# A convolution mixer taken by two halves of the tokens, with one of six convolution tiles moved off TensorE and half of its second product in whole fp32

## The chip, the core and the metric

The kernel runs on one core of one Trainium2 chip. The metric is the device time of one execution in microseconds; the median of several runs counts. Everything is in fp32, with fp32r (one pass through TensorE instead of several) for the large products.

## The reference, cut to what matters

The reference is a trunk of four layers on 256 tokens of 1024 channels. Each layer adds a token mixer and then a squared-ReLU feed-forward network (FFN) of 4096. Only the mixer of layer 1, a Conformer convolution module, is changed:

```
h = xn @ pw1_w + pw1_b
a, gate = split(h, 2);  h = a * sigmoid(gate)
h = causal depthwise convolution of width 31 (h, dw_w) + dw_b
h = layer_norm(h, ln_w, ln_b)          # over the 1024 channels of a token
h = silu(h)
x = x + h @ pw2_w + pw2_b
x = x + squared_relu_mlp(rms_norm(x))  # the FFN of layer 1 follows
```

## The kernel before

Activations lie channels on partitions: eight tiles of 128 channels by 256 tokens. Weights come from memory in chunks of 1 MB, two units of 128 x 1024 to a chunk, through three buffers (`raw`). `unit` splits a unit into a high fp32r part (a copy on ScalarE, line 350) and the rest (a subtraction on VectorE, line 351). A product is then three fp32r matmuls for each pair of a weight block and an activation tile (lines 470 to 472 in `mm_b`): high by high, high by low, low by high. Activations are split in the same way (`split`, lines 362 and 363).

The mixer is `conv`. After the first product and the gate, the eight gated tiles (`hc`) stand in SBUF with 31 columns of zeros ahead. Their depthwise convolution is done in two ways:

- Tile 0 on VectorE, one fused multiply-add for each of 31 taps (line 982); tile 1 on ScalarE (a scaled copy for each tap, line 989) with GpSimd adding (line 991). Both are over before TensorE begins its own tiles.
- Tiles 2 to 7 on TensorE (`taps_pe`, line 995). `spread` writes two tiles at a time to a scratch in device memory (`hd`, line 912) and reads them back so that 32 channels by 4 shifts lie on the 128 partitions (line 915, into a `raw` buffer). Thirty-two matmuls in fp32, each of 32 columns of weights by 256 tokens, then make a tile; four of them stand side by side in the array's columns.

For the layer norm, each finished tile gets a common shift taken off (line 1045) and is squared on ScalarE (line 1004). `stats` sums tiles 0 to 5 by channels with 32-column matmuls (line 1009); `cols` then turns the sums and tiles 6 and 7 into a column for each token (line 387). Mean and scale are worked out in small VectorE steps, and `bcast` (line 394) spreads them over the partitions again. `warm` puts idle bf16 matmuls on TensorE meanwhile (line 291). `swish` normalizes on VectorE (lines 1100 and 1101) and applies SiLU on ScalarE (line 1103). The second product is `out_proj`, and its results are added to `x` (line 868), from which `norm_pair` makes the FFN's inputs `z` (line 418).

Order: within this stage PE, DVE, ACT and POOL keep the order in which the code is written (`manual_schedule`); elsewhere a scheduler decides. All DMAs are issued from SP's queue, in order. The release of `raw` buffers sets when weights load: all three hold `spread` tiles during the taps.

Of the kernel before, what the change touches and what calls it, by code (L numbers as in the profile page):

```python
# [39 lines left out]
PET = (2, 3, 4, 5, 6, 7)  # L40
DVT = (0, 1)
# [200 lines left out]
class Trunk:  # L242
# [81 lines left out]

    def unit(self, key, after=None):
# [19 lines left out]
        with ExitStack() as stack:  # L345
            for i in after or ():
                stack.enter_context(self.tc.issue_after(i.ins))
            for i in range(0, 1024, n):
                s = slice(i, i + n)
                nc.scalar.copy(hi[:, s], src[:, s])  # L350
                nc.vector.tensor_sub(lo[:, s], src[:, s], hi[:, s])  # L351
        self.un += 1
        return hi, lo

# [4 lines left out]
    def split(self, src, eng="act"):  # L359
        nc = self.nc  # L360
        o = self.bigt(F32R)
        (nc.scalar.copy if eng == "act" else nc.vector.tensor_copy)(o[:, :S], src)  # L362
        self.last_lo = nc.vector.tensor_sub(o[:, S:], src, o[:, :S])
        return o
# [177 lines left out]
    def res_pairs(self, name, l, acts, nkb, group, evac, before=None, after=None):  # L542
        for g in range(4 // group):
            ps = [self.acc() for _ in range(group)]
            for kb in range(nkb):
                if before is not None:
                    before(kb)
                for p in range(group):
                    w = self.unit((name, l, "b", kb, (g * group + p) * 256), after and after.pop(0))
# [305 lines left out]
    def out_proj(self, name, l, y, nkb, group, nxt, bias=None, before=None, after=None):  # L855
        nc = self.nc

        acts = lambda k: y[k]
# [15 lines left out]
        self.res_pairs(name, l, acts, nkb, group, evac, before, after)  # L874
# [16 lines left out]
    def conv(self, j, nxt):  # L891
# [17 lines left out]
        def spread(d):  # L909
            rows = self.dram.tile([2, 4, 32, HL], F32, name=self.nm("hd"), tag="hd")  # L910
            for i in range(2):
                nc.sync.dma_start(rows[i].rearrange("j c u -> (j c) u"), hc[d + i][:, :HL])
            t = self.raw.tile([P, RAWW], F32, name=self.nm("raw"), tag="raw")
            for s in range(4):
                nc.sync.dma_start(
                    v3(t[32 * s : 32 * s + 32], 8, HW),
                    rows.rearrange("i j c u -> c (i j) u")[:, :, NG * s : NG * s + HW],
                )
            for i in range(2):
# [40 lines left out]
        spread(6)  # L960
        self.table("silu_and_others")
        tap = lambda t, w: hc[t][:, w + 1 : w + 1 + S]
# [4 lines left out]
        halves = lambda t: (t()[:, :S], t()[:, :S])  # L967
        r0, r1 = halves(self.mis), halves(self.bigt)
        pb, pbs = {}, [self.acc() for _ in range(3)]
        for i, d in enumerate(PET):  # L970
            pb[d] = pbs[i % 3][:, (i // 3) * S : (i // 3 + 1) * S]


        def tap_dve(t, w, a, first=False, bias=False):
            if bias:
                nc.vector.tensor_scalar(
                    out=a, in0=tap(t, w), scalar1=wc(t, w), scalar2=db(t), op0=ALU.mult, op1=ALU.add
                )
            elif first:
                nc.vector.tensor_scalar(out=a, in0=tap(t, w), scalar1=wc(t, w), scalar2=None, op0=ALU.mult)  # L980
            else:
                nc.vector.scalar_tensor_tensor(out=a, in0=tap(t, w), scalar=wc(t, w), in1=a, op0=ALU.mult, op1=ALU.add)

        def tap_pool(t, w, a, first=False, bias=False):
            pr = a if first else self.prp.tile([P, S], F32, name=self.nm("pr"), tag="pr")
            if bias:
                nc.scalar.activation(out=pr, in_=tap(t, w), func=AF.Identity, scale=wc(t, w), bias=db(t))
            else:
                nc.scalar.activation(out=pr, in_=tap(t, w), func=AF.Copy, scale=wc(t, w))
# [13 lines left out]
        def square(d):  # L1003
            L["sq", d] = nc.scalar.activation(out=cc[d][:, S:], in_=cc[d][:, :S], func=AF.Square)

        def stats(*ds):
            for d in ds:
                o = 32 * (d % 4)
                nc.tensor.matmul(L["st"][o : o + 32], self.c("o32", 32), cc[d], start=d < 4, stop=d in (2, 3, 4, 5), **kw)


        def cols(src, sc, es=(0, 1), first=False, last=False):
            for e in es:
                for t in range(2):
                    i = t * 2 + e
                    self.colsum(
                        L["sc"][:, i : i + 1], src[:, e * S + t * P : e * S + (t + 1) * P], self.sc(sc),
                        first and i == 0, last,
                    )
# [10 lines left out]
        def shift_b():  # L1030
            s0 = self.col(2, "lns")
            nc.vector.tensor_copy(s0, L["ps"][:, :2])
            L["s"] = self.bcast(s0, "Gb")
            L["st"] = self.mis()
# [9 lines left out]
        def fin_pe(d):  # L1044
            L["fin", d] = nc.vector.scalar_tensor_tensor(
                out=cc[d][:, :S], in0=pb[d], scalar=db(d), in1=L["s"], op0=ALU.add, op1=ALU.subtract
            )
            square(d)

        with self.tc.manual_schedule(engines=MANUAL):  # L1050
# [4 lines left out]
            taps_pe(2)  # L1055
            shift_a()
            taps_pe(3)
            shift_b()
            shift_c()
            square(1)  # L1060
            fin(0, *r0)
            square(0)
            fin_pe(2)
            fin_pe(3)
            taps_pe(4)
            fin_pe(4)
            taps_pe(5)
            fin_pe(5)
            stats(0, 1, 2, 3)
            taps_pe(6)  # L1070
            fin_pe(6)
            stats(4, 5)
            sm, L["sc"] = self.tmp(), self.mis()
            nc.scalar.copy(sm, L["st"])
            taps_pe(7)
            fin_pe(7)
            cols(sm, 128, first=True)
            cols(cc[6], 1024)
            cols(cc[7], 1024, (0,))
            cols(cc[7], 1024, (1,), last=True)  # L1080

            mean, msq = v3(L["sc"][:, :4], 2, 2)[:, :, 0], v3(L["sc"][:, :4], 2, 2)[:, :, 1]
            mc, m2, m = self.col(2, "lnc"), self.col(2, "lnm2"), self.col(2, "lnm")
            nc.vector.tensor_copy(mc, mean)
            self.warm(2)
            mb = self.bcast(mc, "lnb", 1)
            self.warm(2)
            nc.vector.tensor_mul(m2, mc, mc)
            nc.vector.scalar_tensor_tensor(out=m, in0=msq, scalar=EPS, in1=m2, op0=ALU.add, op1=ALU.subtract)
            rs = self.rsqrt(m, 2, "v")  # L1090
            rsb = self.bcast(rs, "lnr", 1)
            self.warm(9)
            y, yp = [], {}

            def swish(d):
                c = cc[d][:, :S]
                if d % 4 == 0:
                    for e in range(d, d + 4):
# [219 lines left out]
```

## Time and profile before

| | us |
|---|---|
| median of 3 runs | 1375.63 (1375.15 to 1376.71) |
| the profiled execution | 1373.77 |
| its span, first to last instruction | 1372.0 |
| TensorE busy in the span | 1357.4 (99%) |
| VectorE busy | 978.4 (71%) |
| ScalarE busy | 770.9 (56%) |
| GpSimd busy | 136.0 (10%) |

An fp32 matmul stands in the profile as two records, so that a tile of 32 tap matmuls shows as x64. TensorE's records overlap: from start to start of two neighbours is what one costs, and it is shorter than a record's own duration. "PEclk" is the granted TensorE clock as a share of 2.4 GHz. The convolution's part that is changed lies between 438 and 512 us of the span.

### The profile page before, as it was taken

To read this page: it belongs to the slowest core of one execution; us is meant where nothing else is said; L and a number is where in the kernel's file an instruction comes from. 1 tells how busy PE (TensorE), PEld (TensorE's weight loads), DVE (VectorE), ACT (ScalarE), POOL (GpSimd) and SP (SyncE) were. 2 spreads that over 40 slices of the span, in tenths; PEclk is the share of its full clock that TensorE was granted. 3 is DMA by queue.
4 is the path that set the end of the run, shared out by engine and by line. 5 is a ranking of instruction groups with operands and counts; after the bars stand their busy time and mean duration, and the time that the engine had idled before them with its cause. 6 is when DMAs were issued, how large, how long until landed. Compare 5 with 4: busy or idle time off the path is not lost.

```text
span 1372.0 us, 22537 instructions
## 1 busy us (share of the span) xinstructions
PE 1357.4 (99%) x9057; PEld 1224.0 (89%) x9058; DVE 978.4 (71%) x1653; ACT 770.9 (56%) x1155; POOL 136.0 (10%) x125
## 2 busy tenths in 40 slices
PE   9999999999999989999999999999999999999998
PEld 7889998888999678888988898888988999988888
DVE  6967778775678588765588587756597687888543
ACT  7545556664456366654568666644565554655442
POOL 2201002000227010000000010000120010100011
PEclk9999999999999999999999999999999999999999
DMA  8543445555455555555543345555554444455550
GB/s 304 210 166 141 152 163 202 184 190 195 170 183 121 160 191 192 196 185 184 184 156 142 133 159 184 197 196 185 182 179 165 150 158 171 168 193 188 191 187 37
DMA packets 38649, 239.93 MB, mean 175 GB/s; under 512 B 4240, under 2 KB 8720, under 8 KB 10896
## 3 DMA queue, kind: packets, MB, share of 16 engines
q1 hardware_dynamic: 38256, 237.97, 49.8%
q8 instruction: 71, 1.16, 0.3%
q10 hardware_dynamic: 288, 0.52, 0.1%
q14 instruction: 34, 0.28, 0.1%
HBM read 236.54 MB, written 1.93 MB: 174 GB/s over the span
## 4 chain that ended last, share of the span: by engine, by line
PE 96%; DVE 2%; DMA 1%; ACT 1%; issue 0%; SPq 0%; POOL 0%; ACTq 0%; DVEq 0%; POOLq 0%
PE acc L497 32%; PE acc L498 16%; PE acc L472 9%; PE acc L470 9%; PE acc L471 9%; PE acc L887 4%; PE acc L886 4%; PE acc L888 4%; PE acc L995 2%; PE mis L387 1%; DMA raw<-in_w 1%; PE mis L394 1%; DVE wl L351 1%; PE acc L486 1%; PE acc L484 1%; PE acc L485 1%
## 5 line engine op out<-in xcount | busy, mean ns | idle before, releaser
L351 DVE TENSOR_TENSOR wl<-raw,wh 128x1024 fp32r<-128x1024 f32 (+1 forms) x444 | 552.1, 1247 | 283.2 <-ACT wh L350 278.1
L350 ACT CAST wh<-raw 128x1024 fp32r<-128x1024 f32 (+1 forms) x444 | 460.6, 1041 | 428.1 <-PE acc L497 207.4
L497 PE MATMUL acc<-z,wh 128*128 128x512 f32 x1120 | 391.8, 395 | 4.1 <-DVE z L418 4.1
L498 PE MATMUL acc<-z,wl 128*128 128x256 f32 x1120 | 312.6, 281 | 0.0
L497 PE MATMUL acc<-big,wh 128*128 128x512 f32 x768 | 267.7, 393 | 0.0
L497 PEld LDWEIGHTS acc<-z,wh 128*128 128x128 f32 x1120 | 209.2, 187 | 52.3 <-DVE z L418 5.2
L498 PE MATMUL acc<-big,wl 128*128 128x256 f32 x768 | 215.2, 280 | 0.0
L498 PEld LDWEIGHTS acc<-z,wl 128*128 128x128 f32 x1120 | 211.6, 189 | 1.0
L497 PEld LDWEIGHTS acc<-big,wh 128*128 128x128 f32 x768 | 143.8, 187 | 32.7
L472 PE MATMUL acc<-big,wl 128*128 128x256 f32 x576 | 162.1, 283 | 0.6 <-DVE wl L351 0.6
L471 PE MATMUL acc<-big,wh 128*128 128x256 f32 x576 | 161.6, 283 | 0.0
L470 PE MATMUL acc<-big,wh 128*128 128x256 f32 x576 | 160.5, 284 | 0.0
L472 PE MATMUL acc<-z,wl 128*128 128x256 f32 x512 | 145.2, 284 | 0.5 <-DVE wl L351 0.5
L470 PE MATMUL acc<-z,wh 128*128 128x256 f32 x512 | 145.4, 284 | 0.0
L498 PEld LDWEIGHTS acc<-big,wl 128*128 128x128 f32 x768 | 145.2, 189 | 0.0
L471 PE MATMUL acc<-z,wh 128*128 128x256 f32 x512 | 144.9, 283 | 0.0
L433 POOL TENSOR_TENSOR t<-t,t 128x512 f32<-128x512 f32 x25 | 38.3, 1532 | 763.5 <-DVE z L418 459.8
L472 PEld LDWEIGHTS acc<-big,wl 128*128 128x128 f32 x576 | 110.3, 192 | 0.8 <-DVE wl L351 0.8
L471 PEld LDWEIGHTS acc<-big,wh 128*128 128x128 f32 x576 | 110.3, 192 | 0.0
L470 PEld LDWEIGHTS acc<-big,wh 128*128 128x128 f32 x576 | 109.1, 192 | 0.9 <-DVE big L362 0.4
L472 PEld LDWEIGHTS acc<-z,wl 128*128 128x128 f32 x512 | 98.1, 192 | 0.8 <-DVE wl L351 0.8
L471 PEld LDWEIGHTS acc<-z,wh 128*128 128x128 f32 x512 | 98.1, 192 | 0.0
(243 smaller groups left out, 1821.1 us busy)
## 6 DMA issues: line engine op xcount, KB each, us to landing
raw<-in_w SPq DMA_DIRECT2D x216, 1024.0 KB, 4.8
raw<-in_w SPq DMA_DIRECT2D x8, 512.0 KB, 8.6
raw<-hd SPq DMA_DIRECT2D x12, 263.0 KB, 4.7
x<-in_x SPq DMA_DIRECT2D x4, 256.0 KB, 6.3
hd<-big SPq DMA_DIRECT2D x6, 143.5 KB, 2.2
cst<-in_cst SPq DMA_DIRECT2D x4, 192.0 KB, 5.0
cst<-in_cst SPq DMA_DIRECT2D x1, 548.0 KB, 9.7
out<-t SPq DMA_DIRECT2D x2, 256.0 KB, 2.7
```

What stands on the lines that cost most here:

```text
L350: nc.scalar.copy(hi[:, s], src[:, s])
L351: nc.vector.tensor_sub(lo[:, s], src[:, s], hi[:, s])
L433: (nc.vector if p == 3 and self.quick else nc.gpsimd).tensor_add(a, self.sq, q)
L470: nc.tensor.matmul(o, wh[:, kk, cs], ah, start=st, stop=False, **kw)
L471: nc.tensor.matmul(o, wh[:, kk, cs], al, start=False, stop=False, **kw)
L472: nc.tensor.matmul(o, wl[:, kk, cs], ah, start=False, stop=en, **kw)
L497: nc.tensor.matmul(ps[m], wh[:, kk, cs], a, start=first and kk == 0, stop=False, **kw)
L498: nc.tensor.matmul(ps[m][:, :S], wl[:, kk, cs], a[:, :S], start=False, stop=last and kk == 3, **kw)
L886: nc.tensor.matmul(ps[t], zh[:, s], wh[:, kk], start=k == 0, stop=False, skip_group_check=True)
L887: nc.tensor.matmul(ps[t], zh[:, s], wl[:, kk], start=False, stop=False, skip_group_check=True)
L888: nc.tensor.matmul(ps[t], zl[:, s], wh[:, kk], start=False, stop=k == 7, skip_group_check=True)
L995: nc.tensor.matmul(pb[d][32 * j : 32 * j + 32], strip[d][g // 4][:, ((g % 4) * 4 + j) * 32 : ((g % 4) * 4 + j + 1) * 32], h4[d][:, j * HW ...
```

## The change

All tokens are taken as two halves of 128. Tile 7 leaves TensorE: VectorE computes its first half (`taps_7a`), ScalarE and GpSimd its second (`taps_7b`). The five tiles left on TensorE are computed by halves, all of the first half ahead of most of the second. The layer norm is done for each half by itself, so that the first half's statistics, broadcasts and SiLU are written between the second half's taps, and the second half's between matmuls of the second product. That product's first four k-tiles (the first half of its contraction) are no longer split in fp32r parts: their four weight units come straight from memory into eight 128 x 512 tiles (`unit_raw`), and 64 plain fp32 matmuls of 128 x 128 by 128 tokens (`mm_h`) take the place of 96 fp32r matmuls by 256 tokens. The last four k-tiles stay as they were. The idle matmuls of `warm` in this stage go.

```diff
-PET = (2, 3, 4, 5, 6, 7)
-DVT = (0, 1)
+PET = (2, 3, 4, 5, 6)
+DVT = (0, 1, 7)
...
+    def unit_raw(self, key, tiles):
+        assert PLAN[self.un] == key, (PLAN[self.un], key)
+        o = self.un % UPC * 1024
+        for t in tiles:
+            self.nc.sync.dma_start(t, self.w_d[self.un // UPC][:, o : o + 512])
+            o += 512
+        self.un += 1
+        return tiles
...
+    def bcast_1(self, c, tag):
+        nc = self.nc
+        ps = self.mis()
+        nc.tensor.matmul(ps[:, :P], c.to_broadcast([P, P]), self.id, start=True, stop=True)
+        b = self.bc.tile([P, P], F32, name=self.nm(tag), tag=tag, bufs=1)
+        nc.scalar.copy(b, ps[:, :P])
+        return b
...
-        spread(6)
+        spread(6, 1)
...
-        def taps_pe(d):
-            for g, j in ((g, j) for g in range(NG) for j in range(4)):
+        def taps_pe(d, h, gs=range(NG)):
+            for g, j in ((g, j) for g in gs for j in range(4)):
                 nc.tensor.matmul(
-                    pb[d][32 * j : 32 * j + 32], strip[d][g // 4][:, ((g % 4) * 4 + j) * 32 : ((g % 4) * 4 + j + 1) * 32],
-                    h4[d][:, j * HW + g : j * HW + g + S], start=g == 0, stop=g == NG - 1, **kw,
-                )
+                    pb[d][32 * j : 32 * j + 32, hs(h)],
+                    strip[d][g // 4][:, ((g % 4) * 4 + j) * 32 : ((g % 4) * 4 + j + 1) * 32],
+                    h4[d][:, hs(h, j * HW + g)], start=g == 0, stop=g == NG - 1, **kw,
+                )
...
+        def mm_h(p, kks, h):
+            for kk in kks:
+                w = v3(W[p][kk // 2], 2, 256)
+                for m in range(2):
+                    nc.tensor.matmul(
+                        ps[p][:, m * S : (m + 1) * S][:, hs(h)], w[:, kk % 2, m * P : (m + 1) * P], cc[kk][:, hs(h)],
+                        start=kk == m == h == 0, stop=False, **kw,
+                    )
...
-            taps_pe(2)
+            W = [self.unit_raw(key(0, p), [(self.tmp if p < 2 else self.bigt)() for _ in range(2)]) for p in range(4)]
+            taps_pe(2, 0)
             shift_a()
-            taps_pe(3)
+            taps_7a(range(4))
             shift_b()
...
+            taps_pe(3, 0)
+            shift_bb()
+            taps_7a(range(4, 11))
+            taps_pe(4, 0)
...
+            taps_pe(5, 0)
+            fin_pe(0, 5)
...
+            taps_pe(2, 1)
+            stats(0, 0, 1, 2, 3)
...
+            taps_pe(3, 1)
+            fin_pe(1, 3)
+            taps_7b(range(21, 23))
+            taps_pe(6, 0)
+            fin_pe(0, 6)
+            taps_pe(4, 1, range(4))
+            stats(0, 4, 5, 6, 7)
+            stats_out(0)
+            taps_7b(range(23, CW))
+            taps_pe(4, 1, range(4, NG))
+            cols_st(0, True)
+            mean_in(0)
+            taps_pe(5, 1, range(4))
+            mean_out(0)
+            scale_in(0)
+            swish_mean(0, 0, 1, 2, 3)
+            fin_7(1)
+            taps_pe(5, 1, range(4, NG))
+            stats(1, 0, 1, 2, 3)
+            scale_out(0)
+            fin_pe(1, 4, 5)
+            taps_pe(6, 1, range(4))
+            swish(0, 0, 1, 2, 3)
+            square(7, 1)
+            stats(1, 4, 5, 7)
+            stats_out(1)
+            taps_pe(6, 1, range(4, NG))
+            swish_mean(0, 4, 5, 6, 7)
+            fin_pe(1, 6)
+            swish(0, 4, 5)
+            ps = [self.acc() for _ in range(4)]
+            mm_h(0, range(2), 0)
+            cols_st(1, False)
+            mm_h(0, range(2, 3), 0)
+            cols_tile(1, 6, True)
+            mean_in(1)
+            mm_h(0, range(3, 4), 0)
+            mm_h(1, range(2), 0)
+            mean_out(1)
+            scale_in(1)
+            W1 = [self.unit(key(1, 0))]
+            swish_mean(1, 0, 1, 2, 3)
+            swish(0, 6, 7)
+            mm_h(1, range(2, 4), 0)
+            mm_h(2, range(3), 0)
+            scale_out(1)
+            mm_h(2, range(3, 4), 0)
+            mm_h(3, range(4), 0)
+            swish(1, 0, 1, 2, 3)
+            W1.append(self.unit(key(1, 1)))
+            for p in range(4):
+                mm_h(p, range(4), 1)
+            swish_mean(1, 4, 5, 6, 7)
+            swish(1, 4, 5, 6, 7)
+        evac = self.out_begin(nxt, "pw2b")
+        for p in range(4):
+            self.mm_b(ps[p], W1.pop(0) if W1 else self.unit(key(1, p)), lambda k: y[k], 4, False, True)
+            evac(p, ps[p])
```

Three places show how instructions move. First SP's queue, from the last two `spread` calls on. Before, the queue there was:

```order
L912 DMA hd_4846<-big_4714 128x287
L912 DMA hd_4846<-big_4717 128x287
L915 DMA raw_4849<-hd_4846 32x8x263 x4
L912 DMA hd_4867<-big_4861 128x287
L912 DMA hd_4867<-big_4864 128x287
L915 DMA raw_4870<-hd_4867 32x8x263 x4
L335 DMA raw_5358<-in_w 128x2048
```

Now it is:

```order
L928 DMA hd_4842<-big_4710 128x287
L928 DMA hd_4842<-big_4713 128x287
L931 DMA raw_4845<-hd_4842 32x8x263 x4
L356 DMA big_5018<-in_w 128x512
L356 DMA big_5019<-in_w 128x512
L356 DMA big_5022<-in_w 128x512
L356 DMA big_5023<-in_w 128x512
L356 DMA t_888_5010<-in_w 128x512
L356 DMA t_889_5011<-in_w 128x512
L356 DMA t_890_5014<-in_w 128x512
L356 DMA t_891_5015<-in_w 128x512
L928 DMA hd_4863<-big_4857 128x287
```

The eight loads of plain weights (line 356) stand ahead of the write and the four reads that spread tile 6; before, nothing stood between them and the spread of tiles 4 and 5.

Second, TensorE where the first half's last tile, 6, is computed (`raw_4865` is its spread tile, `mis_5277` the first half's sums); line 1017 is the tap matmul, 1035 `stats`:

```order
L1017 MATMUL acc_4884<-raw_4837,big_4282 32x128 x16
L1017 MATMUL acc_4883<-raw_4865,big_4292 32x128 x16
L1017 MATMUL acc_4883<-raw_4865,big_4294 32x128 x16
L1017 MATMUL acc_4885<-raw_4845,big_4284 32x128 x16
L1035 MATMUL mis_5277<-big_4875,cst 32x256
L1035 MATMUL mis_5277<-big_4876,cst 32x256
L1035 MATMUL mis_5277<-big_4877,cst 32x256
L1035 MATMUL mis_5277<-big_4878,cst 32x256
```

Before, tile 6 was the fifth of six whole tiles; now its first half is the seventh of ten half tiles, with three half tiles and part of a fourth written behind it on the same queue.

Third, ScalarE after the first half's scale has been broadcast (`lnr`). Line 1027 squares a tile, 1142 is SiLU, 1042 copies the second half's sums out; `big_4878` is tile 7:

```order
L412 COPY lnr_941_5513<-mis_5511 128x128
L1027 ACTIVATE big_4875<-big_4875 128x128
L1027 ACTIVATE big_4876<-big_4876 128x128
L1142 ACTIVATE big_4871<-big_4871,prm 128x128
L1142 ACTIVATE big_4872<-big_4872,prm 128x128
L1142 ACTIVATE big_4873<-big_4873,prm 128x128
L1142 ACTIVATE big_4874<-big_4874,prm 128x128
L1027 ACTIVATE big_4878<-big_4878 128x128
L1042 COPY t_942_5547<-mis_5506 128x256
```

The square of tile 7's second half stands behind four SiLU of the first half; the copy of the second half's sums, which need that square, stands behind it. Nothing of this order was there before: all squares came ahead of the first SiLU.

## Rows read from the trace of the kernel before

**Rows 1.** Busy time by stretch: taps, statistics tail, second product, start of FFN.
```profile
core 0: us, PE busy (x) PEld busy (x) DVE busy (x) ACT busy (x) POOL busy (x), PEclk, DMA share, GB/s
438.60:463.20 24.60, 24.60 (x406) 14.56 (x405) 7.09 (x13) 5.34 (x11) 0.84 (x2) 1.00 0.77 204
463.20:471.40 8.20, 7.99 (x46) 5.80 (x46) 4.75 (x20) 4.98 (x8) 0.00 (x0) 0.79 0.49 167
471.40:495.50 24.10, 23.52 (x193) 23.15 (x192) 17.78 (x33) 11.51 (x20) 0.00 (x0) 1.00 0.37 131
495.50:511.90 16.40, 12.32 (x66) 10.01 (x66) 15.54 (x21) 10.04 (x19) 4.98 (x4) 1.00 0.52 180
```

**Rows 2.** TensorE's timeline, 438 to 472 us: start, duration, instruction, count.
```profile
438.63 3.67 PE L995 MATMUL acc<-raw,big 128*32 128x256 f32 x64
442.23 0.61 PE L387 MATMUL mis<-cst,big 128*128 128x1 f32 x4
442.77 3.67 PE L995 MATMUL acc<-raw,big 128*32 128x256 f32 x64
...
447.00 7.15 PE L995 MATMUL acc<-raw,big 128*32 128x256 f32 x128
453.97 1.04 PE L1009 MATMUL mis<-big,cst 128*32 128x512 f32 x8
454.83 3.64 PE L995 MATMUL acc<-raw,big 128*32 128x256 f32 x64
...
464.10 1.93 PE L387 MATMUL mis<-cst,big 128*128 128x1 f32 x16
...
471.39 0.74 PE L470 MATMUL acc<-big,wh 128*128 128x256 f32 x4
```

**Rows 3.** TensorE's timeline at the FFN's start: idle time ahead, and its releaser.
```profile
497.97 0.50 PE L497 MATMUL acc<-z,wh 128*128 128x512 f32 x1 [2.44 <-DVE z L418]
```

**Rows 4.** TensorE's timeline in two other layers: fp32 matmuls of other shapes.
```profile
706.29 1.08 PE L1189 MATMUL mis<-big,big 128*128 128x128 f32 x8
...
770.66 0.65 PE L1250 MATMUL mis<-big,big 128*64 128x256 f32 x4
771.10 0.44 PE L1253 MATMUL mis<-big,big 128*64 128x128 f32 x4
771.31 0.65 PE L1250 MATMUL mis<-big,big 128*64 128x256 f32 x4
```

**Rows 5.** SP's queue, 430 to 456 us: the last two spreads and what follows.
```profile
436.24 1.80 SPq L915 DMA_DIRECT2D raw<-hd  x4
440.08 0.81 SPq L912 DMA_DIRECT2D hd<-big  x2
445.42 1.80 SPq L915 DMA_DIRECT2D raw<-hd  x4
```

**Rows 6.** DMA issues of the page: count, KB each, median us to landing.
```profile
raw<-in_w SPq DMA_DIRECT2D x216, 1024.0 KB, 4.8
...
raw<-hd SPq DMA_DIRECT2D x12, 263.0 KB, 4.7
hd<-big SPq DMA_DIRECT2D x6, 143.5 KB, 2.2
```

**Rows 7.** Busy time by stretch, around the last spread's write.
```profile
436.20:443.40 7.20, 7.20 (x101) 5.19 (x104) 3.87 (x10) 2.22 (x4) 2.42 (x4) 1.00 0.91 189
443.40:445.40 2.00, 2.00 (x44) 1.20 (x38) 0.00 (x0) 0.00 (x0) 0.00 (x0) 1.00 0.07 17
```

**Rows 8.** Groups by line and shape: busy time, mean ns of one, idle ahead.
```profile
L1103 ACT ACTIVATE t<-big,prm 128x256 f32<-128x256 f32 x8 | 4.7, 598 | 7.9 <-DVE big L1101 7.9
...
L793 DVE SCALAR_TENSOR_TENSOR big<-mis,ck,cst 128x128 f32<-128x128 f32 x8 | 2.8, 344 | 0.0
...
L382 DVE SCALAR_TENSOR_TENSOR vy<-vt,vy 128x2 f32<-128x2 f32 x9 | 1.4, 161 | 0.3
...
L991 POOL TENSOR_TENSOR big<-big,pr 128x256 f32<-128x256 f32 x29 | 27.2, 973 | 26.6 <-ACT pr L989 26.6
```

More of the change, by code (lines that the diff above doesn't have):

```diff
@@ L344, in unit @@
         n = 512 if self.un < 2 * UPC else 1024
[L345 to L351, printed above, removed]
+        for i in range(0, 1024, n):
+            s = slice(i, i + n)
+            nc.scalar.copy(hi[:, s], src[:, s])
+            nc.vector.tensor_sub(lo[:, s], src[:, s], hi[:, s])
         self.un += 1
         return hi, lo
+    def unit_raw(self, key, tiles):
[6 more added lines that the diff above has]
+        return tiles
     def table(self, name):
@@ L548, in res_pairs @@
                 for p in range(group):
-                    w = self.unit((name, l, "b", kb, (g * group + p) * 256), after and after.pop(0))
+                    w = self.unit((name, l, "b", kb, (g * group + p) * 256))
                     self.mm_b(ps[p], w, acts, kb * 4, kb == 0, kb == nkb - 1)
@@ L1001, in conv, with square, stats @@
         L = {}
-        def square(d):
-            L["sq", d] = nc.scalar.activation(out=cc[d][:, S:], in_=cc[d][:, :S], func=AF.Square)
-        def stats(*ds):
+        def square(d, *h):
+            s = hs(h[0]) if h else slice(0, S)
+            nc.scalar.activation(out=cc[d][:, S:][:, s], in_=cc[d][:, s], func=AF.Square)
+        def stats(h, *ds):
+            if ("st", h) not in L:
+                L["st", h] = self.mis()
             for d in ds:
                 o = 32 * (d % 4)
-                nc.tensor.matmul(L["st"][o : o + 32], self.c("o32", 32), cc[d], start=d < 4, stop=d in (2, 3, 4, 5), **kw)
@@ L1012, in cols @@
[L1012 to L1018, printed above, removed]
-                    )
+                nc.tensor.matmul(
+                    L["st", h][o : o + 32, :S], self.c("o32", 32), v3(cc[d], 2, S)[:, :, hs(h)],
+                    start=d < 4, stop=d >= 4 or h == 1 and d == 2, **kw,
+                )
@@ new lines, in stats_out, with cols, cols_st, cols_tile @@
+        def stats_out(h):
+            L["sm", h] = self.tmp(S)
+            nc.scalar.copy(L["sm", h], L["st", h][:, :S])
+            L["sc", h] = self.mis()
+        def cols(h, src, sc, first=False, last=False):
+            for e in range(2):
+                self.colsum(L["sc", h][:, e : e + 1], src[e], self.sc(sc), first and e == 0, last)
+        def cols_st(h, last):
+            cols(h, [L["sm", h][:, hs(e)] for e in range(2)], 128, first=True, last=last)
+        def cols_tile(h, d, last):
+            cols(h, [cc[d][:, hs(h, e * S)] for e in range(2)], 1024, last=last)
@@ L1042, in fin, with taps_7a, taps_7b, fin_7 @@
             nc.vector.tensor_add(c, c, b)
[L1044 to L1048, printed above, removed]
+        def taps_7a(ws):
+            for w in ws:
+                tap_dve(7, w, r7[0][w % 2], w < 2, w == 0, 0)
+        def taps_7b(ws):
+            for w in ws:
+                tap_pool(7, w, r7[1][w % 2], w < 2, w == 0, 1)
+        def fin_7(h):
+            c, s = cc[7][:, hs(h)], L["s"][:, hs(h)]
+            if h:
+                nc.gpsimd.tensor_add(c, *r7[1])
+                nc.gpsimd.tensor_sub(c, c, s)
+            else:
+                nc.vector.tensor_sub(c, r7[0][0], s)
+                nc.vector.tensor_add(c, c, r7[0][1])
+                square(7, h)
```

165 lines of the change are left out of this document (89 added, 76 removed).

## The prediction

> **What bounds the kernel now.** The page's first part has TensorE busy for 99% of the span, so the sum is made on TensorE alone: whatever shortens its work, or its idle time, shortens the kernel. I read next the windows of the four stretches that the change touches [rows 1]. In the first, the tail of the taps, TensorE is busy all the time. The second, the statistics tail, looks busy too (7.99 of 8.20 us), but with idle matmuls, single-column sums and broadcasts; there the granted clock averages 0.79, so part of it runs at 1.2 instead of 2.4 GHz. The third, the second product, has 0.58 us of idle time in 24.10. The fourth, up to the FFN's fourth unit, has 4.08 (16.40 − 12.32), most of it waits for `z` from VectorE, the longest 2.44 us [rows 3]. Behind 511.9 the order on the engines is as before, so I take every difference between the first tap, 438.6, and there. The profiled execution took 1373.77 us for a span of 1372.0; the median of the runs, 1375.63, is 1.86 above it. I work out a difference against the profiled execution and add it to the median. About 0.2%, 2.75 us, is what a measurement of this kernel can tell from no change.
>
> **Work that changes.** TensorE's timeline gives the prices [rows 2]. Two tiles that run back to back are 128 records in 7.15 us; without the last record's own length, about 0.38, a record costs 6.77 / 126 = 0.0537 us and a tile of 64 records 3.44. A single-column sum costs (1.93 − 0.25) / 15 = 0.112 a record, with 0.25 the estimated length of the last one.
>
> (a) Taps: six tiles, 384 records, 20.6 us, become ten halves, 640 records by 128 tokens. No row shows 32-column matmuls at 128 tokens. The nearest are 64-column fp32 matmuls, side by side in the array as these are, at 256 tokens and at 128 [rows 4]: four records at 256 tokens take 0.44 up to the next start (770.66 to 771.10), four at 128 take 0.21 (771.10 to 771.31). The price there follows the tokens. So I take half, 0.0272, and 640 × 0.0272 = 17.4: −3.2 us. The bounds: no lower than this; if nothing is saved by halving, 640 × 0.0537 = 34.4, or +13.8, part of which would fall into waits that I count below.
>
> (b) Statistics: the second stretch, 8.2 us, goes as such. In its place stand 12 single-column records (1.3 us) and four half broadcasts, 8 records of about 0.11 as in the row with 128-token fp32 matmuls [rows 4], 0.9: −6.0. `stats` becomes 15 half-size matmuls in smaller rounds, which I put at 1.7 instead of 1.4: +0.3.
>
> (c) Taps are cut up by other shapes more often. A piece cut in costs more than its records: tap tile, four sums, tap tile are 4.14 us from start to start (438.63 to 442.77), less 3.44 and 0.45 is 0.25 for two changes of shape. I count eight more such changes: +1.0.
>
> (d) Second product: 96 of its 192 fp32r matmuls, at 23.52 / 193 = 0.122 each [rows 1] 11.7 us, become 64 fp32 matmuls of 128 tokens. This shape is in the trace: eight records take 1.08 us [rows 4], and without the last one's tail some 0.11 each. 64 × 2 × 0.11 = 14.1: +2.4. If the whole 1.08 / 8 counts, it is 17.3, +5.6; if the plain product runs as the 64-column rows do (0.21 / 4 = 0.053), 6.8, −4.9. The shape is the same as in the first row, so I stay there. The loads, their splitting for the first four k-tiles and the splits of `y` leave ScalarE and VectorE; those were under TensorE's work but for the 0.58 us of idle time: −0.6.
>
> (e) Start of the FFN. Before, all groups of the second product came to their end in pairs; now the four accumulators finish one after another, each 24 fp32r matmuls or 2.9 us apart. `x` and its parts in the norm for the first two lie under the last two. Of the 4.08 us of idle time I take 3.8 away; the bounds are 0 and 4.1.
>
> The work alone comes to −3.2 − 6.0 + 0.3 + 1.0 + 2.4 − 0.6 − 3.8 = −9.9 us.
>
> **New waits.** (f1) *Tile 6's spread.* SP's queue issued the four reads of a spread in 1.80 us, the next write 440.08, and the reads behind it at 445.42 [rows 5]. A write lands in 2.2 us by itself [rows 6], but here 5.3 passed, because the reads before it kept the DMA engines busy: their share is 0.91 up to 443.4 and 0.07 in the 2 us after [rows 7]. So what is issued ahead is moved ahead. The change puts eight loads, 2 MB together, between this spread's predecessor and its write. From the page, 1024 KB land in 4.8 and 143.5 in 2.2 [rows 6]: 2.6 us for 880 KB, 3.0 us for 1 MB. Two MB take 6 us from 443.4, until 449.4; the write lands at 451.6; the four reads, issued over 1.3 us and about 3 more, at 455.6 to 455.9. TensorE needs them for the seventh half tile: 438.6 + 6 × 1.74 + the sums, broadcast and changes, 1.4 to 1.9, is 450.4 to 450.9. It waits 4.3 to 5.5; I take 4.5. Behind the waiting matmul on TensorE's queue stand three half tiles that do not need this spread, and all later work. If the loads don't hold the write, the reads are issued at 445.42 and land at 450.1, for 0; the longest that I find is 6.6, with both ends late.
>
> (f2) *End of the second half's sums.* These need the square of tile 7, which ScalarE has behind the first half's broadcast, two squares and four SiLU. A SiLU over 256 tokens takes 0.598, VectorE's operations over 128 take 0.344, small ones 0.161 [rows 8]. From the first half's column sums: nine small steps 1.4, broadcast and its copy 0.7, two squares 0.8, a multiplication 0.34, four SiLU of some 0.45 = 1.8, a square 0.4, and some 1.5 for the passing from engine to engine: about 7 us. TensorE has two and a half pieces of taps, two broadcasts, four sums and their changes of shape beside it, 4.7: a wait of 2.3 (bounds 0 and 4).
>
> (f3) *Second half's first product.* From its column sums the same small steps, two broadcasts, four subtractions, one multiplication and one SiLU, and between them the two copies and two subtractions of the next weight unit and the last two SiLU of the first half: some 9.2 us against 26 matmuls of (d) and the broadcasts, 7.1: +2.0 (0 to 4). (f4) The first fp32r group waits some 0.5 for the split of its `y`.
>
> Waits together +9.3. The sum is −9.9 + 9.3 = −0.6 us: **1375.0 us**. The clock is left out of it: an idle stretch of 4.5 us is longer than any here (2.44 left the granted clock at 1.00 [rows 1, 3]). If TensorE came back from it at 1.2 GHz, that would cost up to 1.7 us, what the second stretch lost of its 8.2 at 0.79.
>
> **Rivals.** *Half-width taps don't halve.* The price of a record has a part that doesn't follow the tokens. For: 32 columns by 128 tokens is the smallest shape in this kernel, and nothing so small is in its trace. Against: the 64-column rows halve exactly [rows 4]. What each 0.01 us more costs is 640 × 0.01 = 6.4, of which the waits of (f1) and (f2) take about half. From 0.037 us a record, 3.1 net, the kernel is slower; at 0.0537 it is some 9 us slower, 1384. Centre 1379. Chance 0.20. By the page "TensorEngine Tiling (Array Packing)" of the Trainium skill, section "Performance Considerations", each matmul carries an overhead of about 60 cycles, and a dimension that is already small should not be tiled further. Taken at 2.4 GHz this is 25 ns, an estimate from that page; were it paid for each record it would stand just under the 27 ns that I take, and paid for weight loads as well it would be 32 us for all taps, near the bound without a gain. No run so far shows which.
>
> *The loads don't hold the spread.* (f1) falls away. For: 2 MB on sixteen DMA engines may share with the write instead of going first. Against: [rows 5, 7]. −0.6 − 4.5 = −5.1, partly lost again where later waits grow (f2, f3): −4.5, 1371.1. Chance 0.24.
>
> *The layer norm's chains are longer than TensorE's work beside them.* GpSimd must add tile 7's second half in 29 steps; the whole-width one took 0.973 [rows 8]. At half of that they fit, at over 0.7 tile 7 is ready after 464 and holds the sums of (f2) by some 3 us: 1378.6 (1 to 6 us slower). Chance 0.13.
>
> **How the numbers follow.** The forecast as summed: 0.43, in itself −3 to +2 (1372.6 to 1377.6). Faster takes the second rival and a little of the forecast, 0.28; slower takes 0.17 of the first rival, 0.08 of the third and a little of the forecast, 0.26; the rest, 0.46, lies within 0.2%. The range 1370.6 to 1380.0 leaves out the lower part of the second rival and the upper part of the first and third, together 0.2.
>
> **What the profile after would show.** For (a): starts of neighbouring tap records 0.027 us apart, and a half tile of 1.74. For (f1): TensorE idle before tile 6's first half for 4 to 5 us, ended by the DMA into its spread tile, and the DMA engines full between 443 and 450. For (b): no stretch at a clock under 1.00 near 466. For (d): a record of the plain product each 0.11. For (e): under 0.5 us of idle time before the FFN's first matmuls. For (f2) and (f3): idle time of about 2 us each before the second half's sums, ended by ScalarE's square, and before the second half's first plain matmul, ended by ScalarE's SiLU. The prediction is wrong if halves cost over 0.037 a record, or if TensorE doesn't stop for tile 6.

## The result and the profile after

The changed kernel is slower: a median of 1378.32 us (1376.35 to 1381.65, 20 runs) against 1374.51 us of the kernel before (20 runs beside them), a ratio of 1.0029, 95% interval 1.0021 to 1.0037, or 2.9 to 5.1 us. The forecast was no change. A second set gave 1.0035 (1.0024 to 1.0046).

The profiled execution took 1379.88 us, its span 1378.1, 6.1 more than before. Where they came from is read by counting TensorE's matmul records through both traces and comparing the times of records with the same number:

| from ... to | before | after | difference |
|---|---|---|---|
| start to first tap matmul | 438.63 | 441.52 | +2.89 |
| first tap to the 73rd matmul record of layer 1's FFN (the stage) | 74.49 | 75.41 | +0.92 |
| from there 816 records on, to near the FFN's end | 141.01 | 143.01 | +2.00 |
| from there to the last matmul | 712.02 | 712.06 | +0.04 |

The first line is chance. It arises in the first 50 us, 2.3 of it behind 39 us, in layer 0, which the change doesn't touch: four profiles with the kernel before's code up to there give 438.63 to 441.70, and those with the changed kernel's give 439.18 to 441.54. (The last 0.2 of the 6.1 us lie behind the last matmul.) The stage and the FFN behind it are left: +2.9 us in this pair of profiles.

The windows of the changed kernel over the stage, over a part of the FFN of layer 1, and over the 6 us in which its clock fell:

```profile
core 0: us, PE busy (x) PEld busy (x) DVE busy (x) ACT busy (x) POOL busy (x), PEclk, DMA share, GB/s
441.52:516.93 75.41, 66.78 (x996) 61.02 (x995) 55.67 (x147) 45.97 (x103) 19.75 (x37) 0.98 0.46 154
560.00:580.00 20.00, 20.00 (x115) 17.32 (x115) 15.63 (x31) 13.53 (x22) 0.00 (x0) 1.00 0.51 178
...
484.00:486.00 2.00, 1.96 (x13) 1.97 (x14) 0.06 (x1) 2.00 (x5) 0.00 (x0) 0.74 0.00 0
486.00:488.00 2.00, 2.00 (x11) 2.00 (x11) 1.90 (x5) 2.00 (x4) 0.00 (x0) 0.50 0.00 0
488.00:490.00 2.00, 2.00 (x18) 2.00 (x17) 2.00 (x5) 1.40 (x2) 0.00 (x0) 0.91 0.77 213
```

The same windows of the kernel before: its own spell at the lower clock, the stage, and the FFN.

```profile
466.00:468.00 2.00, 1.79 (x8) 1.24 (x6) 1.61 (x10) 1.33 (x3) 0.00 (x0) 0.50 0.79 328
468.00:470.00 2.00, 2.00 (x10) 1.29 (x9) 1.62 (x6) 0.49 (x2) 0.00 (x0) 0.66 0.04 8
...
438.63:513.12 74.49, 69.62 (x713) 54.55 (x714) 45.78 (x86) 33.09 (x56) 5.79 (x6) 0.98 0.56 171
560.00:580.00 20.00, 20.00 (x118) 17.62 (x117) 15.10 (x30) 14.46 (x23) 0.00 (x0) 1.00 0.51 177
```

Three things are to be seen. TensorE's idle time in the stage (length less busy) went from 4.87 to 8.63 us. The spell at 1.2 GHz did not go with the statistics tail: it stood at 465.9 to 469.4 and stands at 485.0 to 488.4, and in both kernels costs about 1.7 us ((0.50 + 0.34) × 2 and (0.26 + 0.50 + 0.09) × 2). And in the FFN the same 20 us hold 115 matmuls instead of 117 or 118, with TensorE busy all the time and the granted clock at 1.00. What is left of the stage after idle time and clock is work: 67.9 before, 65.1 after.

TensorE's timeline in the changed stage, which answers to [rows 2]:

```profile
446.70 0.71 PE L400 MATMUL mis<-cst,lns 128*128 128x128 f32 x4 [0.79 <-DVE lns L1085]
...
449.04 4.48 PE L1017 MATMUL acc<-raw,big 128*32 128x128 f32 x148 [0.31 <-issue]
...
457.25 2.84 PE L1017 MATMUL acc<-raw,big 128*32 128x128 f32 x96 [1.43 <-DMA raw<-hd]
...
462.85 0.41 PE L1035 MATMUL mis<-big,cst 128*32 128x256 f32 x2 [2.35 <-ACT big L1027]
...
468.39 0.46 PE L410 MATMUL mis<-cst,vy 128*128 128x128 f32 x2 [0.62 <-DVE vy L388]
...
471.96 0.40 PE L1035 MATMUL mis<-big,cst 128*32 128x256 f32 x1 [1.12 <-ACT big L1027]
...
477.29 1.06 PE L1159 MATMUL acc<-big,t 128*128 128x128 f32 x8
478.18 1.50 PE L1159 MATMUL acc<-big,big 128*128 128x128 f32 x12
...
484.04 5.47 PE L1159 MATMUL acc<-big,t 128*128 128x128 f32 x32 [1.90 <-ACT big L1142]
489.34 3.74 PE L1159 MATMUL acc<-big,big 128*128 128x128 f32 x32
```

The waits in brackets sum to 8.5 us. The longest, 2.35, was in no term of the prediction. The plain product runs at (478.18 − 477.29) / 8 = 0.111 us a record, but at (489.34 − 484.04) / 32 = 0.166 behind the idle 1.90. SP's queue and ScalarE's timeline show what stood ahead of three of these waits:

```profile
439.12 2.05 SPq L356 DMA_DIRECT2D big<-in_w  x4
441.22 3.61 SPq L356 DMA_DIRECT2D t<-in_w  x4
445.14 0.33 SPq L928 DMA_DIRECT2D hd<-big  x1
451.65 1.75 SPq L931 DMA_DIRECT2D raw<-hd  x4
```

```profile
459.74 0.31 ACT L1027 ACTIVATE big<-big 128x128 f32<-128x128 f32 x1 [2.95 <-DVE big L1114]
459.95 1.82 ACT L1011 ACTIVATE pr<-big,prm 128x128 f32<-128x128 f32 x5
461.68 0.29 ACT L1027 ACTIVATE big<-big 128x128 f32<-128x128 f32 x1
461.88 0.72 ACT L1011 ACTIVATE pr<-big,prm 128x128 f32<-128x128 f32 x2
462.51 0.29 ACT L1027 ACTIVATE big<-big 128x128 f32<-128x128 f32 x1
...
481.00 0.49 ACT L1141 ACTIVATE big<-big,prm 128x128 fp32r<-128x128 f32 x1 [2.30 <-DVE big L1136]
...
482.84 0.24 ACT L412 COPY lnr<-mis 128x128 f32<-128x128 f32 x1
483.49 1.65 ACT L1142 ACTIVATE big<-big,prm 128x128 f32<-128x128 f32 x4 [0.41 <-DVE big L1136]
```

The write of tile 6's spread took 6.5 us up to its reads (445.14 to 451.65). The square that the first half's sums wait for, at 462.51, stands behind seven scaled copies for tile 7's second half, whose sum is needed only at 467.8 us. Just ahead of them ScalarE had been idle for 2.95 us, held by the square of tile 7's first half (459.74), which waits for VectorE: five of the copies could have run in that time, had they been written ahead of that square. The copy of the second half's scale (`lnr`, 482.84) stands behind four SiLU of the first half that are needed 10 us later.

### The profile page after: what moved, and what is told of

Its sections match the earlier page's. It is cut to its first block, busy times and chain, and to the rows that moved or that the text cites. A ratio compares the mean times of both kernels' runs of the same rounds, so it can differ in the third digit from the quotient of the medians.

```text
span 1378.1 us, 23268 instructions
## 1 busy us (share of the span) xinstructions
PE 1359.6 (99%) x9339; PEld 1233.6 (90%) x9339; DVE 985.8 (72%) x1709; ACT 784.1 (57%) x1203; POOL 146.3 (11%) x154
## 4 chain that ended last, share of the span: by engine, by line
PE 94%; DVE 3%; ACT 2%; issue 1%; POOL 0%; DMA 0%; SPq 0%; ACTq 0%; DVEq 0%; POOLq 0%
PE acc L511 32%; PE acc L512 16%; PE acc L486 8%; PE acc L484 8%; PE acc L485 8%; PE acc L903 4%; PE acc L902 4%; PE acc L904 4%; DVE mis L1004 1%; PE acc L1159 1%; PE mis L393 1%; PE acc L500 1%; PE acc L498 1%; PE acc L499 1%; PE mis L400 1%; PE mis L799 1%
## 5 line engine op out<-in xcount | busy, mean ns | idle before, releaser
L347 DVE TENSOR_TENSOR wl<-raw,wh 128x1024 fp32r<-128x1024 f32 (+1 forms) x440 | 544.5, 1240 | 285.8 <-ACT wh L346 282.0
L512 PE MATMUL acc<-big,wl 128*128 128x256 f32 x768 | 215.4, 280 | 0.0
L511 PEld LDWEIGHTS acc<-big,wh 128*128 128x128 f32 x768 | 144.0, 187 | 33.8
L486 PE MATMUL acc<-big,wl 128*128 128x256 f32 x544 | 153.5, 283 | 0.0
L485 PE MATMUL acc<-big,wh 128*128 128x256 f32 x544 | 153.3, 283 | 0.0
L484 PE MATMUL acc<-big,wh 128*128 128x256 f32 x544 | 153.1, 284 | 0.0
L512 PEld LDWEIGHTS acc<-big,wl 128*128 128x128 f32 x768 | 145.1, 189 | 0.0
L485 PEld LDWEIGHTS acc<-big,wh 128*128 128x128 f32 x544 | 104.2, 192 | 0.0
L486 PEld LDWEIGHTS acc<-big,wl 128*128 128x128 f32 x544 | 104.2, 192 | 0.0
L484 PEld LDWEIGHTS acc<-big,wh 128*128 128x128 f32 x544 | 103.6, 192 | 0.5 <-issue 0.3
```

What stands on the lines that cost most here:

```text
L484: nc.tensor.matmul(o, wh[:, kk, cs], ah, start=st, stop=False, **kw)
L485: nc.tensor.matmul(o, wh[:, kk, cs], al, start=False, stop=False, **kw)
L486: nc.tensor.matmul(o, wl[:, kk, cs], ah, start=False, stop=en, **kw)
L511: nc.tensor.matmul(ps[m], wh[:, kk, cs], a, start=first and kk == 0, stop=False, **kw)
L512: nc.tensor.matmul(ps[m][:, :S], wl[:, kk, cs], a[:, :S], start=False, stop=last and kk == 3, **kw)
```

## Experiments

**The same two kernels again** (no edit).

> The changed kernel as it is, profiled a second time. In its first profile three things lie beside the stage's own work: TensorE at 1.2 GHz near 45 us, in the first layer (some 2.9 us later than in the kernel before, ahead of anything that was changed); TensorE at 1.2 GHz for about 4 us after an idle stretch of 1.90 us in the second product; and pairs of FFN matmuls 1.5% further apart from 553 to 662 us, with the granted clock at 1.00 (2 us). Theory A (the change makes the last two): both recur in this profile, the first need not, and the ratio is 1.003. Theory B (all three come and go by chance): at least one of the last two is missing here, and the time of this execution is lower by the 1.8 to 2 us that each is worth.

> The kernel before as it is, profiled a second time. Theory A (the change makes the slower pace of the FFN behind the stage): no stretch of 1.5% further apart matmuls between 500 and 660 us here either, ratio 1.000. Theory B (by chance): such a stretch may stand here, or the first layer may lose 2.9 us near 45 us.

Measured: `after_again` 1.0035 (1.0024 to 1.0046), `before_again` 1.0001 (0.9992 to 1.0009). The changed kernel's stage took 75.75 us, with 8.73 idle and the clock low from 483.3 to 486.7; its 816 FFN records 143.54. The kernel before had 74.34, with 4.42 idle and its low clock at the FFN's start (500.7 to 504) instead of the tail, and 141.20. So theory A holds for stage and FFN, and the clock is no difference between these two pairs of profiles: each has one such spell, not always at the same place. It is not in every execution: `e_flip_b` below, whose stage is that of the kernel before, has none there (74.09 us, 5.66 idle).

**The second half's scale ahead of ScalarE's other work.**

```diff
-            W1 = [self.unit(key(1, 0))]
             swish_mean(1, 0, 1, 2, 3)
-            swish(0, 6, 7)
...
             swish(1, 0, 1, 2, 3)
-            W1.append(self.unit(key(1, 1)))
+            swish(0, 6, 7)
+            W1 = [self.unit(key(1, 0))]
...
             swish(1, 4, 5, 6, 7)
+            W1.append(self.unit(key(1, 1)))
```

> The changed kernel with the last two SiLU of the first half and the split of the next weight unit written behind the second half's first four SiLU, so that the broadcast of the second half's scale is not held behind them. Theory A (that wait of 1.90 us and the half clock that follows it, some 1.8 us, are what the stage lost against the forecast): both go, 3 to 3.7 us faster than the changed kernel, less what a new wait at the fp32r products takes (0 to 1.5): ratio to the kernel before near 1.001. Rival (the waits only move, ScalarE has the same work): under 1 us gained, ratio 1.0025 to 1.003.

Measured: 1.0007 (0.9998 to 1.0016), about 3.8 us less than the changed kernel's 1.0035 beside it. The time is near the one expected, but the profile gives another sum. The wait and the low clock are gone, yet the stage fell only from 75.75 to 74.29:

```profile
441.43:515.72 74.29, 66.12 (x995) 59.51 (x995) 56.38 (x146) 45.54 (x103) 19.86 (x37) 1.00 0.47 155
560.00:580.00 20.00, 20.00 (x117) 17.48 (x116) 15.32 (x30) 13.37 (x22) 0.00 (x0) 1.00 0.59 207
```

Idle time is 8.17 us: of the 1.90, 1.27 came back in two waits, 0.44 for the next weight split and 0.83 for `z` at the FFN's start. The other 2.3 us came from the FFN (141.26 for the 816 records), which has 117 matmuls in 20 us here. Nothing in its code had been edited, but the scheduler's order of TensorE in it is another one from its 176th record to its 273rd. The last place where two matmuls of 512 columns follow each other is its 269th record in the changed kernel and its 237th here:

```profile
550.43 0.62 PE L511 MATMUL acc<-z,wh 128*128 128x512 f32 x2
```

```profile
543.96 0.63 PE L511 MATMUL acc<-z,wh 128*128 128x512 f32 x2
```

What such a place does to the spacing is tested further below.

**Tile 7's copies away from the squares.**

```diff
             taps_7a(range(24, CW))
+            taps_7b(range(16, 21))
             fin_7(0)
-            taps_7b(range(16, 21))
...
-            taps_7b(range(21, 23))
...
-            taps_7b(range(23, CW))
+            taps_7b(range(21, CW))
```

> The changed kernel with seven of ScalarE's copies for tile 7's second half written behind, or ahead of, the three squares that the first half's sums wait for. Theory: the 2.35 us for which TensorE waits for the square of tile 6 are ScalarE's queue; about 2 us go, and the second half's tile 7 still is in time (ratio 1.0015). Rival: GpSimd's chain then ends later, and the second half's sums wait for it longer than the 1.1 us of now: nothing gained, 1.003.

Measured: 1.0009 (1.0001 to 1.0018). The stage took 72.92 us:

```profile
439.20:512.12 72.92, 65.36 (x995) 59.55 (x995) 56.29 (x147) 46.31 (x104) 19.94 (x37) 1.00 0.48 160
```

The wait for the square is gone (idle 7.56 instead of 8.63 to 8.73; some of it came back in small waits), and so is the low clock, although the 1.90 us ahead of the second half's product still stand. The theory holds; with the clock the stage is 2.5 to 2.8 us shorter, of which the idle time is 1.1 to 1.2. The 816 FFN records take 143.54 us, as in the second profile of the changed kernel, and their order is the changed kernel's.

**Tile 6's spread ahead of the loads.**

```diff
...
-            W = [self.unit_raw(key(0, p), [(self.tmp if p < 2 else self.bigt)() for _ in range(2)]) for p in range(4)]
+            with self.tc.issue_after(L_sp[0].ins):
+                W = [self.unit_raw(key(0, p), [(self.tmp if p < 2 else self.bigt)() for _ in range(2)]) for p in range(4)]
```

`L_sp[0]` is the last read of tile 6's spread.

> The changed kernel with the eight loads of plain weights issued behind tile 6's spread on SP's queue instead of ahead of it. Theory (these loads hold the spread): TensorE's wait for the spread tile, 1.4 to 1.6 us in two profiles of the changed kernel, goes; the time falls by as much only if the wait for the square of tile 6 behind it does not take it up again (that square waits for ScalarE's queue, whose copies are paced by other things): 0 to 1.5 us gained, ratio to before 1.002 to 1.0035. Rival (the reads wait for something else, such as the write's own latency): the wait stays above 1 us.

Measured: 1.0038 (1.0024 to 1.0052), no gain. SP's queue shows the mechanism that the prediction named, write to reads 2.0 us instead of 6.5:

```profile
444.42 0.34 SPq L930 DMA_DIRECT2D hd<-big  x1
446.46 1.73 SPq L933 DMA_DIRECT2D raw<-hd  x4
```

But TensorE waits at the same place for something else:

```profile
447.40 5.50 PE L1019 MATMUL acc<-raw,big 128*32 128x128 f32 x192
452.71 0.62 PE L1037 MATMUL mis<-big,cst 128*32 128x256 f32 x8
...
456.34 1.09 PE L1019 MATMUL acc<-raw,big 128*32 128x128 f32 x32 [1.25 <-DVE big L1121]
458.97 1.97 PE L1019 MATMUL acc<-raw,big 128*32 128x128 f32 x64 [1.54 <-issue]
```

The first two rows are three half tiles back to back, (452.71 − 447.40) / 192 = 0.0277 us a record. The first wait is for VectorE's last step on tile 2's second half, whose accumulator tile 6 shares. The second wait is time in which the profile shows no wait. The stage is 75.47 us, with 8.70 idle: the spread's wait lay over another one.

**All orders mended**, without and with the loads behind the spread. Beside the two edits of ScalarE's order, `shift_b()` stands ahead of `taps_7a(range(4))`, `square(7, 1)` ahead of `swish(0, 0, 1, 2, 3)`, and the second half's tiles 4 to 7 around the first weight split.

> All orders that were mended one by one, together: the three squares ahead of ScalarE's copies, tile 7's square ahead of the first half's SiLU, the common shift's copy ahead of tile 7's taps on VectorE, the second half's scale and SiLU ahead of the last SiLU of the first half and of the weight split. The same work on every engine. Theory (the stage lost by the order of single instructions on ScalarE and VectorE): first tap to the FFN's fourth unit falls from 75.4 to 75.7 us to 69 to 71, and the kernel is 3.5 to 5 us faster than before, if the matmuls of layer 1's FFN are at their closer spacing, 2 us less if they are not. Rival (the chains are bound by the amount of work on ScalarE and VectorE): 73 us or more, ratio about 1.000.

> The kernel of the run before this one, with the loads of plain weights behind tile 6's spread as well. Theory: 1 to 1.5 us less in the stage than without. Rival: the next weights come later by as much, and the wait reappears at the fp32r products or at the FFN's start: no difference.

Measured: 0.9986 (0.9977 to 0.9995) and 0.9990 (0.9981 to 0.9999), so both are faster than the kernel before, and the loads make no difference. The windows of the stage and TensorE's waits in the first of them:

```profile
441.27:512.70 71.43, 66.17 (x995) 59.70 (x995) 56.72 (x146) 45.82 (x103) 18.88 (x37) 1.00 0.47 160
```

```profile
448.83 4.48 PE L1017 MATMUL acc<-raw,big 128*32 128x128 f32 x148 [1.20 <-issue]
...
456.67 2.84 PE L1017 MATMUL acc<-raw,big 128*32 128x128 f32 x96 [1.06 <-DMA raw<-hd]
460.41 0.41 PE L1035 MATMUL mis<-big,cst 128*32 128x256 f32 x2 [0.48 <-ACT big L1027]
```

With the same operations as the changed kernel the stage is 4.0 to 4.3 us shorter and 2.9 to 3.1 shorter than before. It is a little longer than the 69 to 71 expected. Neither has a spell at the lower clock in the stage, and the 816 FFN records take 141.29 us in both, with the order of `e_scale`.

**The spacing of the FFN's matmuls.** The FFN's matmuls come in pairs of a wide one (512 columns) and a narrow one (256). `mm_w` now writes two neighbouring pairs as wide, wide, narrow, narrow at chosen places, and nothing else changes; `swap`, 0 elsewhere, is the number of such exchanges in a weight unit.

```diff
...
+            if kk < swap:
+                for m in range(2):
+                    nc.tensor.matmul(ps[m], wh[:, kk, m * P : (m + 1) * P], a, start=first and kk == 0, stop=False, **kw)
+                for m in range(2):
+                    nc.tensor.matmul(ps[m][:, :S], wl[:, kk, m * P : (m + 1) * P], a[:, :S], start=False, stop=last and kk == 3, **kw)
+                continue
```

> The changed kernel; only in the second product of layer 1's FFN eight pairs of neighbouring matmuls are exchanged (wide, wide, narrow, narrow in place of wide, narrow, wide, narrow), at five places. The work, its operands and its DMAs are the same. Theory A (the wider spacing is a phase of TensorE's stream of matmuls that an irregular place in the order sets or ends): the spacing of pairs, 352 ns on the mean in both profiles of the changed kernel up to 660 us, falls to 347 behind at least one of the places. Theory B (it is a state of the engine, such as a throttle, that the load before it brings on): 352 throughout.

> The kernel before with the same eight exchanges in the second product of layer 1's FFN as in the changed kernel before. Its pairs are at 347 ns there. Theory: one exchange makes it 352, two leave it, one makes it 347, one 352, three 347: the mirror image of the other run. Rival (the wider spacing belongs to the changed kernel): 347 throughout.

Each of the two ran once, for its profile, and no time is read from it. The rows are the first exchange at each of the five places, ahead of which 48, 32, 32 and 32 pairs lie; first the changed kernel, then the kernel before:

```profile
601.45 0.64 PE L511 MATMUL acc<-big,wh 128*128 128x512 f32 x2
...
618.11 0.63 PE L511 MATMUL acc<-big,wh 128*128 128x512 f32 x2
...
629.21 0.63 PE L511 MATMUL acc<-big,wh 128*128 128x512 f32 x2
...
640.50 0.63 PE L511 MATMUL acc<-big,wh 128*128 128x512 f32 x2
...
651.60 0.62 PE L511 MATMUL acc<-big,wh 128*128 128x512 f32 x2
```

```profile
595.90 0.63 PE L497 MATMUL acc<-big,wh 128*128 128x512 f32 x2
...
612.55 0.62 PE L497 MATMUL acc<-big,wh 128*128 128x512 f32 x2
...
623.65 0.62 PE L497 MATMUL acc<-big,wh 128*128 128x512 f32 x2
...
634.95 0.63 PE L497 MATMUL acc<-big,wh 128*128 128x512 f32 x2
...
646.05 0.62 PE L497 MATMUL acc<-big,wh 128*128 128x512 f32 x2
```

In the changed kernel the pairs stand 353 ns apart up to 601 us (115 matmuls in 20 us, as above), then 16.66 / 48 = 347, 11.10 / 32 = 347, 11.29 / 32 = 353 and 11.10 / 32 = 347. Two neighbouring pairs written in another order end the wider spacing, and another such exchange brings it back, so theory A holds against a throttle. In the kernel before the same distances are 16.65, 11.10, 11.30 and 11.10. That it would be a mirror image is refuted: the first exchange leaves 347 there and ends 353 here. Behind an exchange the spacing is the same in both kernels; the place decides it, not the spacing ahead of it.

> The changed kernel with one single exchange of two neighbouring matmuls (wide, wide, narrow, narrow in place of wide, narrow, wide, narrow), in the tenth column pair of the first product of layer 1's FFN. In the run with eight exchanges an odd number at a place changed the spacing of all pairs behind it and an even number did not. Theory (the spacing is one of two phases of the stream of matmuls; an exchange changes it): from that place, near 558 us, to the FFN's end the pairs stand 347 instead of 352 ns apart, some 1.6 us for nothing; the stage stays at 75.4 to 76.5; ratio to before near 1.002. Rival: unchanged, 1.003.

> The kernel before with one such exchange in layer 3's FFN, where its pairs stand 352 ns apart from 1213 to 1339 us in every profile. Theory: 347 ns behind it, 1.8 to 2 us faster (ratio 0.9987): what the changed kernel lost in layer 1's FFN is nothing of its own, since as much can be had or lost anywhere by the order of two matmuls. Rival: no change, 1.000.

Measured: `e_flip` 1.0026 (1.0015 to 1.0037), `e_flip_b` 0.9988 (0.9979 to 0.9997). With one exchange near 557 us the changed kernel has, behind it,

```profile
560.00:580.00 20.00, 20.00 (x117) 17.47 (x116) 14.96 (x28) 13.39 (x21) 0.00 (x0) 1.00 0.60 211
```

and its 816 FFN records take 141.64 us, 1.4 to 1.9 less than in the two profiles of the changed kernel; the stage is unchanged, 75.81. The difference of the medians is too small for the interval to show it. In the kernel before, the exchange in layer 3 brings the part behind layer 1 from 712.02 to 709.72 us, 2.3 less, and the time agrees within its interval (0.4 to 2.9 us less):

```profile
1225.00:1245.00 20.00, 20.00 (x117) 17.47 (x116) 17.42 (x31) 11.42 (x19) 0.00 (x0) 1.00 0.57 206
```

where the kernel before has

```profile
1225.00:1245.00 20.00, 20.00 (x115) 17.36 (x114) 17.29 (x33) 11.63 (x20) 0.00 (x0) 1.00 0.48 161
```

**The version that beats both**: the mended orders and the exchange in layer 3.

> The changed kernel with the mended orders on ScalarE and VectorE (ratio 0.9986 by itself), and one exchange of two matmuls in layer 3's FFN. Theory: the two add up, 1.9 us more than without the exchange: some 4 us faster than the kernel before, ratio 0.997. Rival: no more than 0.9986.

Measured: 1370.85 us, 0.9975 (0.9965 to 0.9985), 2.1 to 4.8 us faster than the kernel before. Its stage is 71.23 us, the part behind layer 1 709.71: the two gains add up.

## Why the prediction was wrong

The step that failed is the sentence that the order of instructions behind 511.9 us is as before and that every difference is therefore taken up to there. Two errors are in it. The scheduler's order of TensorE agrees in the two kernels only from about 547 us (551 in the changed one) on. And behind that place, with the same matmuls in the same order, TensorE was not equally fast: pairs stood 353 instead of 347 ns apart up to 662 us. That is 2.0 us in the first profile and 2.3 to 2.5 in the second, over half of the 3.8 us between the medians. `e_flip` takes 1.4 to 1.9 of it away without touching work or waits, and `e_flip_b` takes 2.3 from another layer of the kernel before. The first error seems to have made the second: all profiles with the changed kernel's order up to 551 us (`after`, `after_again`, `e_square`, `e_spread`, and `e_pace` and `e_flip` up to their first exchange) stand at 353 behind it, and all with the order of `e_scale` (also `e_all`, `e_all_spread` and `e_best`) at 347, as do those with the order of the kernel before. No run changed the order ahead of 551 us alone.

The other part, 0.9 to 1.4 us, lies in the stage, which was forecast at −0.6. Its measured column is the first pair of profiles:

| | forecast | measured |
|---|---|---|
| work | −3.8 (−9.9 less 4.4 of idle time and 1.7 of low clock in it) | −2.8 |
| idle time | +4.9 (+9.3 − 4.4) | +3.8 |
| low clock | −1.7, as a part of the tail | 0.0 |
| sum | −0.6 | +1.0 |

That the idle time came within 1.1 us of its forecast is luck: (f1) was 3.1 us too high, and waits of 3.45 us that were not in the sum (2.35, 0.79 and 0.31) took its place. Of the work, (a) is 0.3 of the missing 1.0; no run separates the rest by term.

By its steps:

- (a) was right: 0.0277 us a record where nothing disturbs it, 17.7 for all. The first rival, half taps that don't halve, falls. Of the overhead of some 60 cycles for each matmul that the page "TensorEngine Tiling (Array Packing)" of the Trainium skill gives in "Performance Considerations", the runs show that matmul and weight load don't pay it one after the other (50 ns, an estimate from that page); 27.7 ns is just above one payment, so whether it would bind below 128 tokens no run here shows.
- (b) took the whole tail as gained, its low clock too, and left the clock out of the new stage; its one row on that was 2.44 us of idle time that left it at 1.00. The spell of 1.2 GHz came back behind the idle 1.90. This was named as an open cost of up to 1.7 us, and it is this size, though behind another wait than the one it was named for.
- (d) and (e) were right: 0.111 us a record, and no idle time left at the FFN's start (4.08 before).
- (f1) named the right mechanism with the wrong price: TensorE waited 1.4 to 1.6 us, not 4.5 (by the forecast's own times it is 4.7 to 5.5). Less the 2.89 us of the start, the reads were issued at 448.8 (forecast 451.6) and TensorE came at 452.9 (forecast 450.4 to 450.9), late by the 0.79 us below and others. And with the loads away VectorE holds the same matmul. Of the three half tiles behind it one, tile 6's second half, needs the same spread; there is no part of a fourth.
- Not in the sum: 2.35 us for tile 6's square behind tile 7's copies on ScalarE, and 0.79 for the common shift behind tile 7's taps on VectorE. The orders of ScalarE and VectorE around the first half's sums had not been followed row by row, only those around the second half's.
- (f2) was 1.12 + 0.62 + 0.10 = 1.8 (forecast 2.3), (f3) 1.90 (2.0), (f4) nothing (0.5).

The rival of longer layer-norm chains was nearest, but not by the cause that it named: GpSimd's adds took 0.42 us each (seven in 2.92) and fit, and it was ScalarE's queue, ahead of the first half's sums and not the second's. What the halves could bring is seen in `e_all`: 3 us in the stage, once the same instructions are written in another order on ScalarE and VectorE.

## What to carry to other kernels

When a stage is cut into halves that run beside each other, follow every in-order engine row by row at each hand-over, the first half's too: instructions that nobody waited for yet, ahead of ones that TensorE waited for, cost 4 us of the stage here, with the clock spell behind them (`e_all`), more than the 2.8 us of work saved. Compare two traces by the same matmuls, up to the end of the program and not just up to the end of the edit: a difference can lie where nothing was edited, because the scheduler has written other instructions in another order. And before a small loss is put down to a change, see whether a reordering that does no work brings it back.

## What the runs showed of the hardware that was not expected

- Alternating fp32r matmuls of 512 and 256 columns have two spacings, 347 and 353 ns a pair, at a granted clock of 1.00 and with the same durations on VectorE and ScalarE. Each lasts for tens of us (553 to 662 us in the first profile of the changed kernel, 1213 to 1339 in the kernel before), and an exchange of two neighbouring matmuls can end or start it. Why a place gives one or the other stays open; the spacing ahead of the place does not decide it.
- The length of an idle stretch alone doesn't tell whether the clock falls behind it. In the changed kernel 2.35 us left it at 1.00 and 1.90 us was followed by 1.2 GHz; in `e_pace` 2.47 us at the place of the 2.35 was followed by 6.8 us of it (463.4 to 470.2) and the 1.90 by none; in `e_square` the 1.90 was followed by none either. The 2.44 us ahead of the FFN in the kernel before, which left the clock at 1.00 in the first profile, were followed by 1.2 GHz from 500.7 to 504.1 us in `before_again`.
